# The FFN's up projection by one level of Strassen's scheme, with a separate down projection, in a float32 decoder layer on one core

## The chip, the cores and the metric

One Trainium2 chip; the kernel runs on one of its cores. The metric is the device time of one execution in microseconds (us). A core has five engines that work side by side, each through its own queue and strictly in that queue's order: TensorE (PE, with PEld for its loads of stationary tiles), VectorE (DVE), ScalarE (ACT), GpSimd (POOL) and SyncE (SP), which here only issues DMAs. SBUF holds tiles of 128 partitions; matmuls write to PSUM, which has banks of 512 float32 columns in a partition.

## The reference, cut to what matters

The reference is a decoder layer with two mixer branches, cross attention and a gated convolutional FFN, for 1024 tokens of 1024 channels, float32. The change touches the last part only (`D_FF` is 2816, so `w_up` is 1024 x 5632):

```python
def _conv_ffn(h, w_up, conv_w, conv_b, w_down):
    u = _causal_dwconv(h @ w_up, conv_w, conv_b)
    a, b = jnp.split(u, 2, axis=-1)
    return (jax.nn.gelu(a) * b) @ w_down
...
        h = _rmsnorm(x, f_norm_g[l])
        x = x + _conv_ffn(h, f_w_up[l], f_conv_w[l], f_conv_b[l], f_w_down[l])
    return _rmsnorm(x, final_norm_g)
```

The convolution is causal over three tokens, for each channel by itself.

## The kernel before

Activations lie channel-major: a tile has 128 channels in the partitions and the 1024 tokens (T) in the free dimension, so 1024 channels are 8 K tiles (KD). A float32 product is made of three passes of a faster type: both factors are split into a high part (a cast on ScalarE, L176) and a low part (the difference, on VectorE or GpSimd, L177), and a matmul group computes high x high, high x low and low x high (`gemm_part`, L202). One instruction takes a stationary tile of 128x128 and a moving tile of 128x512. `ntile` makes one 128-column tile of a product with K = 1024: 8 K tiles x 3 passes x 2 halves of the tokens, 48 matmuls. `load_w` loads a weight tile of 512 KB through SyncE's queue into WR and splits it into WH and WL (two buffers each) or into a pool that is passed in; its low parts go to VectorE and GpSimd in turn (`low`).

SBUF is shared out by pools that all stages take tiles from: S (24 tiles of 128x1024), R (4), Z (3), Y (18 of about 128x512), VV (4). PSUM has psM, two tiles of two banks, and psA, four of one bank.

The output projection of the attention and the second residual are in `resid` (L872): for each K tile n the projection, two additions to x2 (halves of the tokens), the scaled split of x2 into the FFN's moving tiles x2g (in S, R and pairs of Y), and the sum of squares for the norm. The norm's factor by token, r3, is not multiplied into x2g; it is computed while the first up tile runs (`rstd_col`, L229 on VectorE and L230 on GpSimd), broadcast over the partitions by matmuls (`bcast_col`, L236) and applied to each up tile as it leaves PSUM.

The FFN goes through 22 (NF) pairs of channel tiles, f of the first half and NF + f of the second. `up_conv` runs `ntile`, multiplies PSUM by rb3 (L1044, VectorE), starts the convolution on ScalarE (L1045) and adds its two other taps on VectorE (L1047). `ups` takes the gelu (L1057), multiplies the halves on GpSimd (L1059) and splits the product, the hidden tile. Hidden tiles stay in SBUF. Chunks of two hidden tiles (FCH) are followed by their share of the down projection (`downs`: `down_tile` and an addition of PSUM to x2, L1080), so that up and down tiles alternate; the down weights' splits lie in VV. The last four hidden tiles are taken with the final norm by token spans (`span_sum`, `span_norm`), the tail.

The kernel's instructions are handed to a scheduler (`schedule_with_timeline_sim=True`), which decides the order of each engine's queue before the kernel runs; the order of the code is only its input.

Of the kernel before, what the change touches and what calls it, by code (L numbers as in the profile page):

```python
# [10 lines left out]
F32 = mybir.dt.float32  # L11
# [8 lines left out]
P = 128  # L20
# [23 lines left out]
NZ = 3  # L44
# [3 lines left out]
# the order of the first part: p, r S5's parameters and runs; v values, g gates, j projections, m heads, s splits  # L48
# of the mLSTM; a merge of its share; y loads of S5's outputs
# [5 lines left out]
# the order of the cross attention's projections: k, v, q  # L55
# [30 lines left out]
def hybrid_layer(ctx: ExitStack, tc: tile.TileContext, a):  # L86
# [69 lines left out]
    # the tensor engine's clock rises with use: products of zeros until the first inputs are in  # L156
# [7 lines left out]
    class Halves:  # L164
        """Two [128, 512] tiles in the place of one [128, 1024]."""
# [30 lines left out]
    def gemm_part(ps, wk, xh, xl, width, first, last):  # L196
        """ps[:, :width] += w^T x for one K tile; wk = (hi, lo) stationary [128, 128]."""
        wh, wl = wk
        spans = [(s, min(s + 512, width)) for s in range(0, width, 512)]
        for lhsT, rhs, is_first, is_last in ((wh, xh, True, False), (wh, xl, False, False), (wl, xh, False, True)):  # L200
            for s, e in spans:
                PE.matmul(ps[:, s:e], lhsT, rhs[:, s:e], start=first and is_first, stop=last and is_last)  # L202
# [10 lines left out]
    def rstd_col(sq, n, out, more=()):  # L213
        """out[:, j] = (sum over partitions of sq at token j*128+p, / n + eps)^-1/2; sq: halves; more: further addends."""
        ntt = out.shape[1]
        t = small([P, 8], "ms", 2)
        if more:
            # a bank for each column, so that the last addend is all that is left at the end
# [6 lines left out]
        else:  # L225
            ps = psA()
# [5 lines left out]
    def bcast_col(cvec, halves):  # L232
        """halves[i][m, j*128+p] = cvec[p, 4i+j] for every m (PSUM banks)."""
# [5 lines left out]
    def rstd_bc(rcol, out):  # L239
        h = [psA(), psA()]  # L240
# [54 lines left out]
    for j in range(4):  # L295
# [3 lines left out]
        # block step reversed, so that x is (channel, step) rows in the order of the powers  # L299
# [12 lines left out]
    def acc_exp(dst, x, tmp):  # L312
        """dst = exp(x) to float32's accuracy; tmp: four slices of x's width and one of integers."""
# [22 lines left out]
    def sincos(cos_out, sin_out, f, t1, t2):  # L336
        """cos/sin of f turns, |f| a little over 1/2 at most, by half angles."""
# [7 lines left out]
    def cmul(e, re, im, ar, ai, br, bi, t1, t2):  # L345
        """(re, im) = (ar, ai) * (br, bi)"""
# [7 lines left out]
    # b and c, [128 = (group of pair, state), pair, channel]; the imaginary part of c negated  # L354
# [7 lines left out]
    # powers a^0 .. a^8: real, imaginary, negated imaginary part  # L362
# [25 lines left out]
    # turns of theta (m = 1) and of 8 theta (m = 8): leading part, small rest  # L388
# [33 lines left out]
    # input coefficient (a - 1) / lambda  # L422
# [33 lines left out]
    def s5_params(qi):  # L456
# [8 lines left out]
        # a^j b, j = 0..7, and conj(c a^j), j = 1..8  # L465
# [15 lines left out]
        # impulse response Re(c a^j b), with d at j = 0, to DRAM behind seven zero blocks  # L481
# [22 lines left out]
        # state to output, rows (real, imaginary) x state of one group  # L504
# [8 lines left out]
    def s5_run(qi, abt, es):  # L513
# [8 lines left out]
        # rotation by 8 theta per block  # L522
# [7 lines left out]
        # block inputs  # L530
# [7 lines left out]
        # rotate back to one phase, scan over blocks, rotate forward  # L538
# [25 lines left out]
        # outputs, [128 blocks, (step, channel)]  # L564
# [51 lines left out]
    def gate_rows():  # L616
# [48 lines left out]
        # emt = exp(-(bcum + M)) in ls, iw = exp(m_prev - M) in xf, w = exp(a + g - m_new) in ig, -M in cmax  # L665
# [48 lines left out]
        # chunk states, the normaliser as the last column  # L714
# [27 lines left out]
        # scores  # L742
# [6 lines left out]
        # output gates by token  # L749
# [6 lines left out]
        # numerators, with the denominator as the last column; gated numerators and their sums of squares  # L756
# [183 lines left out]
    def v_step(pv, k):  # L940
        """One K tile of the token-major values."""
# [81 lines left out]
    def alloc_x2(n):  # L1023
        if n < 4:
            return (S, R)[n // 2](F32R), (S, R)[n // 2](F32R)
        return Halves([Y(F32R), Y(F32R)]), Halves([Y(F32R), Y(F32R)])

    x2, x2g, sq2 = resid(a["w_o"], oT, lambda n: x1[n], "f_g", alloc_x2)
# [227 lines left out]
```

## Time and profile before

| | us |
|---|---|
| device time, three runs | 1744.49, 1749.63, 1749.22 |
| median | 1749.22 |
| span of the profiled execution | 1743.6 |
| mean time of L1044 (x44), L1059 (x22) | 1.224, 2.399 |
| load of an up weight tile, 512 KB | 3.3 |
| mean DMA rate over the span | 63 GB/s |

The page gives the span of the profiled execution, from its first instruction to its last, and no device time beside it; the fastest run is 0.9 us longer than this span, the median 5.6. In the rows below, a line is "start, duration, engine, line, operation, output<-inputs, shape, xcount", and square brackets hold how long the engine had idled and what released it. In rows of groups, the numbers behind the bar are busy microseconds in all, mean nanoseconds of one, and idle time just before them with what ended most of it. Such an idle time counts only on an engine that others wait for.

### The profile page before, as it was taken

The page shows a single profiled execution, that of the slowest core. Times are in us where ns is not written, and L with a number is a line of the kernel's source. Part 1 is how long each engine was busy: PE and PEld are TensorE (multiplying, and loading weights), DVE is VectorE, ACT ScalarE, POOL GpSimd, SP SyncE. Part 2 cuts the span into 40 slices and gives each one's busy share as a digit, 9 for nine tenths or more (in the row PEclk, how much of TensorE's full clock was granted, in tenths as well). Part 3 has the DMA queues.
Part 4 walks back from the last instruction along what each step waited for, and adds up shares of the span by engine and source line. Part 5 has one row for each costly group of instructions (what it writes and reads, how often), then busy time and mean ns, then how long its engine had stood idle before and what let it go on. Part 6 is the DMA issues. An engine that isn't in the chain of part 4 may idle for free. (4 is left out here: it accounts for less than half of the span.)

```text
span 1743.6 us, 20590 instructions
## 1 busy us (share of the span) xinstructions
PE 1711.3 (98%) x8435; PEld 1433.4 (82%) x8435; DVE 881.6 (51%) x1261; ACT 594.4 (34%) x895; POOL 351.5 (20%) x215
## 2 busy tenths in 40 slices
PE   9889999999999999999999999999999999999997
PEld 7788888888888888888888888888888888888887
DVE  8776766565243333623563545453453454454445
ACT  5345654544342222523452333222122122222223
POOL 2352323321022211000001122121121121121125
PEclk9899999999999999999999999999999999999999
DMA  5231321113111212223101111111111111111102
GB/s 182 88 93 39 99 72 55 45 57 112 44 61 43 84 62 97 97 80 115 61 1 49 48 51 59 48 45 53 49 36 61 48 36 61 49 37 61 49 12 97
DMA packets 46142, 110.59 MB, mean 63 GB/s; under 512 B 5024, under 2 KB 19040, under 8 KB 46048
## 3 DMA queue, kind: packets, MB, share of 16 engines
q1 hardware_dynamic: 42544, 101.24, 17.9%
q10 hardware_dynamic: 3504, 8.04, 1.3%
q8 instruction: 66, 1.08, 0.3%
q14 instruction: 28, 0.23, 0.0%
HBM read 100.35 MB, written 8.91 MB: 63 GB/s over the span
## 5 line engine op out<-in xcount | busy, mean ns | idle before, releaser
L202 PE MATMUL M<-S,WH 128*128 128x512 f32 (+1 forms) x2184 | 582.7, 384 | 0.0
L202 PEld LDWEIGHTS M<-S,WH 128*128 128x128 f32 x2184 | 403.5, 188 | 80.2 <-issue 0.3
L202 PE MATMUL M<-S,WL 128*128 128x512 f32 (+1 forms) x1124 | 347.9, 384 | 0.0
L176 ACT CAST WH<-WR 128x1024 fp32r<-128x1024 f32 (+2 forms) x143 | 137.2, 960 | 547.8 <-PE M L202 462.3
L177 POOL TENSOR_TENSOR WL<-WR,WH 128x1024 fp32r<-128x1024 f32 (+2 forms) x60 | 124.8, 2080 | 942.6 <-ACT WH L176 927.3
L202 PEld LDWEIGHTS M<-S,WL 128*128 128x128 f32 x1124 | 210.5, 188 | 40.8 <-DVE WL L177 0.2
L202 PE MATMUL M<-Y,WH 128*128 128x512 f32 x832 | 231.5, 393 | 0.0
L202 PE MATMUL M<-S,VV 128*128 128x512 f32 (+1 forms) x924 | 213.5, 390 | 0.0
L202 PEld LDWEIGHTS M<-S,VV 128*128 128x128 f32 x924 | 170.6, 188 | 40.5 <-DVE S L1080 2.0
L202 PEld LDWEIGHTS M<-Y,WH 128*128 128x128 f32 x832 | 156.2, 188 | 35.2
L1044 DVE TENSOR_TENSOR S<-M,Z 128x1024 f32<-128x1024 f32 x44 | 53.9, 1224 | 216.3 <-PE M L202 207.4
L177 DVE TENSOR_TENSOR WL<-WR,WH 128x1024 fp32r<-128x1024 f32 (+2 forms) x83 | 98.8, 1190 | 99.4 <-ACT WH L176 99.3
L1047 DVE SCALAR_TENSOR_TENSOR S<-S,cols,S 128x1023 f32<-128x1023 f32 x88 | 120.6, 1372 | 23.1 <-ACT S L1045 21.9
L1080 DVE TENSOR_TENSOR S<-S,M 128x512 f32<-128x512 f32 x144 | 93.1, 682 | 60.6 <-PE M L202 60.6
L202 PE MATMUL M<-Y,WL 128*128 128x512 f32 x352 | 109.6, 392 | 0.0
L202 PE MATMUL M<-R,WH 128*128 128x512 f32 x368 | 99.0, 389 | 0.0
L202 PEld LDWEIGHTS M<-R,WH 128*128 128x128 f32 x368 | 69.1, 188 | 14.3
L202 PEld LDWEIGHTS M<-Y,WL 128*128 128x128 f32 x352 | 66.0, 188 | 15.2
L176 ACT CAST S<-S 128x1024 fp32r<-128x1024 f32 x22 | 23.1, 1050 | 130.4 <-POOL S L1059 130.4
L1059 POOL TENSOR_TENSOR S<-S,S 128x1024 f32<-128x1024 f32 x22 | 52.8, 2399 | 64.6 <-DVE S L1047 64.6
L1045 ACT ACTIVATE S<-S,cols 128x1024 f32<-128x1024 f32 x44 | 54.8, 1245 | 31.6 <-DVE S L1044 31.6
L883 DVE TENSOR_TENSOR S<-S,M 128x512 f32<-128x512 f32 x32 | 20.6, 684 | 85.5 <-PE M L202 85.5
(397 smaller groups left out, 2124.1 us busy)
## 6 DMA issues: line engine op xcount, KB each, us to landing
WR<-in_w_up_dram SPq DMA_DIRECT2D x44, 512.0 KB, 3.3
WR<-in_w_in_dram SPq DMA_DIRECT2D x29, 512.0 KB, 3.3
WR<-in_w_down_dram SPq DMA_DIRECT2D x22, 512.0 KB, 3.2
Y<-Rd SPq DMA_DIRECT2D x16, 256.0 KB, 5.2
WR<-in_w_br_dram SPq DMA_DIRECT2D x16, 256.0 KB, 2.7
WR<-in_w_out_dram SPq DMA_DIRECT2D x8, 512.0 KB, 3.7
S<-in_xT_dram ACTq DMA_DIRECT2D x8, 512.0 KB, 3.3
WR<-in_w_q_dram SPq DMA_DIRECT2D x8, 512.0 KB, 3.3
```

The source lines that it names most:

```text
L176: A.copy(out=hi, in_=src)
L177: (lo_eng or V).tensor_tensor(out=lo, in0=src, in1=hi.bitcast(F32), op=ALU.subtract)
L202: PE.matmul(ps[:, s:e], lhsT, rhs[:, s:e], start=first and is_first, stop=last and is_last)
L883: V.tensor_tensor(out=xj, in0=xj, in1=ps[:, hs], op=ALU.add)
L1044: V.tensor_tensor(out=raw, in0=ps, in1=rb3, op=ALU.mult)
L1045: A.activation(out=acc, in_=raw, func=AF.Identity, scale=col("fcw", 3 * ct + 2), bias=col("fcb", ct))
L1047: V.scalar_tensor_tensor(out=acc[:, d_:], in0=raw[:, : T - d_], scalar=col("fcw", 3 * ct + 2 - d_), in1=acc[:, d_:], op0=ALU.mult, op1=ALU ...
L1059: G.tensor_tensor(out=gb, in0=ga, in1=gb, op=ALU.mult)
L1080: V.tensor_tensor(out=xj, in0=xj, in1=ps[:, 512 * j : 512 * j + 512], op=ALU.add)
```

## The change

Strassen's scheme in Winograd's form computes a 2x2 block product with seven products of blocks instead of eight, for more additions. Here the blocks are: the even and the odd K tiles (the inner dimension), the two channel tiles of a pair (f and NF + f), and the two halves of the tokens, H0 and H1. A pair, 96 matmuls before, is seven products of 12 (4 K tiles x 3 passes).

- The right factors X[1..7] of the products are made once from x2 (`factors_even`, `factors_odd`): differences of scaled tiles on VectorE and GpSimd, and the split of each. Product 1's lie in VV, product 5's in R, the others in S.
- The left factors are made for each pair from four blocks of weights: four sums on GpSimd (`sums`), casts on ScalarE and low parts on VectorE, or GpSimd for products 2 and 4 (`weights`). They are prepared seven products ahead; three of the seven slots are pairs of Y tiles, the others halves of WH and WL tiles. The host lays `w_up` out in these blocks.
- The products are combined as they leave PSUM (`product`): a copy on ScalarE, six VectorE passes that read PSUM, and the factor rb3 on VectorE for one quarter and on GpSimd for three (L1148, L1151). `finish` has the convolution, gelu and product of the halves, and writes the hidden tile to DRAM (Gd).
- x2 goes to DRAM (X2d) and comes back when the last pair begins. The down projection is a stage by itself behind all pairs, with hidden tiles and weights loaded one chunk ahead, in nine chunks of two and the unchanged tail.
- Z has six tiles, and the scratch memory of dynamic DMAs is set to 2048 bytes. All comments are gone.

```diff
-NZ = 3
+NZ = 6
...
+    def put(p, i, f, alloc):
+        hi, lo = HL(alloc)
+        A.copy(out=hi, in_=f)
+        (G if p in (1, 3, 5) else V).tensor_tensor(out=lo, in0=f, in1=hi.bitcast(F32), op=ALU.subtract)
+        X[p][i] = (hi, lo)
...
+    class Pair:
+        BANK = {1: 0, 2: 0, 6: 1, 7: 2, 4: 2, 5: 3, 3: 3}
...
+        def sums(self):
+            a11, a21, a22, a12 = self.r0[:, H0], self.r0[:, H1], self.r1[:, H0], self.r1[:, H1]
+            s1, s2, s3, s4 = [Y() for _ in range(4)]
+            G.tensor_tensor(out=s1, in0=a21, in1=a22, op=ALU.add)
+            G.tensor_tensor(out=s2, in0=s1, in1=a11, op=ALU.subtract)
+            G.tensor_tensor(out=s3, in0=a21, in1=a11, op=ALU.subtract)
+            G.tensor_tensor(out=s4, in0=a12, in1=s2, op=ALU.subtract)
+            self.src = {1: a11, 2: a12, 3: s4, 4: a22, 5: s1, 6: s2, 7: s3}
+
+        def weights(self, p):
+            k = wslot[0] = (wslot[0] + 1) % 7
+            if k in (1, 3, 5):
+                hi, lo = Y(F32R), Y(F32R)
+            else:
+                w = wp.tile([P, T], F32R, tag="WH" if k in (0, 4) else "WL", name=nm("W2"))
+                hi, lo = w[:, H0], w[:, H1]
+            A.copy(out=hi, in_=self.src[p])
+            (G if p in (2, 4) else V).tensor_tensor(out=lo, in0=self.src[p], in1=hi.bitcast(F32), op=ALU.subtract)
+            self.w[p] = (hi, lo)
...
+        def product(self, p):
+            ps = self.bank(self.BANK[p])
...
+            for i in range(4):
+                c = slice(i * P, (i + 1) * P)
+                xh, xl = X[p][i]
+                for lhsT, rhs, f, l in ((wh, xh, p in self.FRESH and i == 0, False), (wh, xl, False, False), (wl, xh, False, i == 3)):
+                    PE.matmul(ps, lhsT[:, c], rhs, start=f, stop=l, skip_group_check=True)
...
+            if p == 1:
+                left["s"] = Y()
+                A.copy(out=left["s"], in_=ps)
+            elif p == 6:
+                left["u2"] = Y()
+                V.tensor_tensor(out=left["u2"], in0=left["s"], in1=ps, op=ALU.add)
+            elif p == 2:
+                V.tensor_tensor(out=self.ra[:, H0], in0=ps, in1=rb3[:, H0], op=ALU.mult)
...
+                    V.tensor_tensor(out=self.rb[:, H1], in0=left["u3"], in1=ps, op=ALU.add)
...
+                    V.tensor_tensor(out=self.ra[:, H1], in0=left["u2"], in1=ps, op=ALU.add)
+                G.tensor_tensor(out=self.ra[:, H1], in0=self.ra[:, H1], in1=rb3[:, H1], op=ALU.mult)
+            if p == 4:
+                V.tensor_tensor(out=self.rb[:, H0], in0=left["u2"], in1=ps, op=ALU.add)
+                G.tensor_tensor(out=self.rb, in0=self.rb, in1=rb3, op=ALU.mult)
...
+            G.tensor_tensor(out=gb, in0=ga, in1=gb, op=ALU.mult)
+            nc.sync.dma_start(out=Gd[self.f], in_=gb)
...
+    STEADY = (1, 6, 7, 5, 2, 4, 3)
...
+    for k, (f, p) in enumerate(jobs):
+        pr = pairs[f]
+        if not pr.have:
+            if f + 2 < NF:
+                pairs[f + 2].load(S)
...
+        if len(pr.have) == 3 and f > 1:
+            for g in (f - 1,) if f > 2 else (0, 1):
+                pairs[g].finish()
+        pr.product(p)
+        weights(k + 7)
+        if k == 1:
+            rstd_col(sq2, D, r3, alloc=psM)
+        elif k == 2:
+            m = psM()
+            rstd_bc(r3, rb3, [m[:, H0], m[:, H1]])
...
+        downs(ws, gs)
+        if c == 0:
+            pairs[NF - 1].finish()
```

The scheduler orders both kernels' queues anew. Three places show how. (A name's number is the buffer; L numbers of the changed kernel are its own: L1120 the products' matmul, L1084 to 1087 the sums, L1098 a low part of weights, L1128, L1137 and L1142 reads of PSUM, L1148 and L1151 the factor rb3, L1157 the convolution, L1165 the product of the halves.) First TensorE around the broadcast of r3 (L236), before, inside the first up tile:

```order
L202 MATMUL M_7768<-Y_7445,WH_7764 128x512
L202 MATMUL M_7768<-Y_7446,WH_7764 128x512
L202 MATMUL M_7768<-Y_7447,WH_7764 128x512
L202 MATMUL M_7768<-Y_7448,WH_7764 128x512
L202 MATMUL M_7768<-Y_7445,WL_7765 128x512
L236 MATMUL A_7743<-ident,r_7674 128x128 x4
L236 MATMUL A_7744<-ident,r_7674 128x128 x4
L202 MATMUL M_7768<-Y_7446,WL_7765 128x512
```

The same place in the changed kernel's TensorE queue, inside a product of pair 0:

```order
L1120 MATMUL A_7814<-S_7791,W_1126_7768 128x512 x3
L1120 MATMUL A_7834<-S_7264,Y_7771 128x512 x2
L1120 MATMUL A_7834<-S_7264,Y_7772 128x512
L1120 MATMUL A_7834<-S_7425,Y_7771 128x512 x2
L1120 MATMUL A_7834<-S_7425,Y_7772 128x512
L236 MATMUL M_7889<-ident,r_7119 128x128 x8
L1120 MATMUL A_7834<-S_7586,Y_7771 128x512 x2
L1120 MATMUL A_7834<-S_7586,Y_7772 128x512
```

The broadcast stands in the middle of a group of matmuls in both. Second, GpSimd's queue in the middle of the FFN, before:

```order
L177 TENSOR_TENSOR WL_9713<-WR_9710,WH_9712 128x1024
L1059 TENSOR_TENSOR S_9626<-S_9564,S_9626 128x1024
L177 TENSOR_TENSOR WL_9961<-WR_9958,WH_9960 128x1024
L1059 TENSOR_TENSOR S_9766<-S_9704,S_9766 128x1024
L177 TENSOR_TENSOR VV_10033<-WR_10030,VV_10032 128x1024
```

GpSimd's queue in the changed kernel, the second part of a round of two pairs that repeats through the up stage:

```order
L1084 TENSOR_TENSOR Y_10062<-WR_9894,S_9895 128x512
L1098 TENSOR_TENSOR W_1527_10003<-S_9746,W_1527_10003 128x512
L1085 TENSOR_TENSOR Y_10063<-Y_10062,WR_9894 128x512
L1086 TENSOR_TENSOR Y_10064<-WR_9894 128x512
L1087 TENSOR_TENSOR Y_10065<-S_9895,Y_10063 128x512
L1165 TENSOR_TENSOR S_9967<-S_9962,S_9967 128x1024
L1098 TENSOR_TENSOR Y_10170<-S_9895,Y_10169 128x512
L1151 TENSOR_TENSOR Z_9900<-Z_9900,Z_7120 128x1024
L1098 TENSOR_TENSOR W_1554_10152<-S_9895,W_1554_10152 128x512
L1148 TENSOR_TENSOR Z_9899<-Z_9899,Z_7120 128x512
L1151 TENSOR_TENSOR Z_10047<-Z_10047,Z_7120 128x1024
L1148 TENSOR_TENSOR Z_10046<-Z_10046,Z_7120 128x512
```

Where GpSimd had low parts and one product of halves, it now has sums, low parts, factors and products of halves of two pairs in one queue, with the factors of both pairs at the end of the round. Third, VectorE's queue in the middle of the FFN, before:

```order
L1044 TENSOR_TENSOR S_8011<-M_7962,Z_7675 128x1024
L177 TENSOR_TENSOR WL_8099<-WR_8096,WH_8098 128x1024
L1047 SCALAR_TENSOR_TENSOR S_8012<-S_8011,cols,S_8012 128x1023
L1047 SCALAR_TENSOR_TENSOR S_8012<-S_8011,cols,S_8012 128x1022
L1044 TENSOR_TENSOR S_8073<-M_8024,Z_7675 128x1024
```

VectorE's queue in the changed kernel, in the same round of two pairs (A and M are PSUM):

```order
L1098 TENSOR_TENSOR W_1516_9923<-WR_9745,W_1516_9923 128x512
L1128 TENSOR_TENSOR Y_9938<-Y_9913,M_9898 128x512
L1098 TENSOR_TENSOR W_1522_9959<-Y_9917,W_1522_9959 128x512
L1098 TENSOR_TENSOR Y_9941<-Y_9916,Y_9940 128x512
L1137 TENSOR_TENSOR Y_9957<-Y_9938,M_9944 128x512
L1098 TENSOR_TENSOR Y_9987<-Y_9915,Y_9986 128x512
L1157 SCALAR_TENSOR_TENSOR S_9962<-Z_9750,cols,S_9962 128x1023
L1157 SCALAR_TENSOR_TENSOR S_9962<-Z_9750,cols,S_9962 128x1022
L1157 SCALAR_TENSOR_TENSOR S_9967<-Z_9751,cols,S_9967 128x1023
L1157 SCALAR_TENSOR_TENSOR S_9967<-Z_9751,cols,S_9967 128x1022
L1098 TENSOR_TENSOR W_1541_10070<-WR_9894,W_1541_10070 128x512
L1142 TENSOR_TENSOR Z_9900<-Y_9957,M_9944 128x512
```

Reads of PSUM, which had two passes of other work between them, now stand among low parts of the next pair's weights and, for both tiles of a pair at once, four convolution passes.

More of the change, by code (lines that the diff above doesn't have):

```diff
@@ new lines, in hybrid_layer, with weights, begin @@
+    pairs = [Pair(f) for f in range(NF)]
+    jobs = [(0, 1), (0, 5), (1, 1), (1, 5), (0, 2), (0, 3), (1, 2), (1, 3), (0, 7), (0, 6), (0, 4), (1, 7), (1, 6), (1, 4)]
+    jobs += [(f, p) for f in range(2, NF) for p in STEADY]
+    wslot = [6]
+    def weights(k):
+        if k < len(jobs):
+            f, p = jobs[k]
+            if not hasattr(pairs[f], "src"):
+                pairs[f].sums()
+            pairs[f].weights(p)
+    def begin():
+        for f in range(2):
+            pairs[f].load(Z)
+            pairs[f].sums()
+        for k in range(7):
+            weights(k)
```

204 lines of the change are left out of this document (137 added, 67 removed).

## The prediction

> **What bounds the kernel now.** I read the page's busy times first, then a table of windows by stage, then single rows of TensorE, VectorE and GpSimd inside the FFN stage.
>
> ```profile
> span 1743.6 us, 20590 instructions
> PE 1711.3 (98%) x8435; PEld 1433.4 (82%) x8435; DVE 881.6 (51%) x1261; ACT 594.4 (34%) x895; POOL 351.5 (20%) x215
> ```
>
> ```profile
> core 0: us, PE busy (x) PEld busy (x) DVE busy (x) ACT busy (x) POOL busy (x), PEclk, DMA share, GB/s
> 200.00:920.00 720.00, 716.29 (x3658) 606.55 (x3658) 343.18 (x533) 285.62 (x504) 115.45 (x79) 1.00 0.22 70
> 920.00:1015.90 95.90, 95.90 (x440) 79.83 (x439) 41.86 (x53) 29.91 (x44) 11.26 (x5) 1.00 0.15 50
> 1015.90:1681.80 665.90, 665.90 (x2898) 542.70 (x2897) 320.44 (x325) 165.24 (x150) 125.88 (x52) 1.00 0.15 49
> 1681.80:1743.60 61.80, 50.85 (x333) 46.10 (x331) 30.44 (x56) 20.29 (x41) 26.99 (x23) 0.94 0.19 69
> ```
>
> The columns are busy microseconds and instructions by engine, then the granted clock. The output projection (920 to 1015.9) and the FFN (to 1681.8) have TensorE busy for all of their 761.8 us at a clock of 1.00. VectorE is busy for 48% of the FFN and GpSimd for 19%. So matmuls set the time, and whatever removes matmuls gains at once, until another engine needs longer than what is left.
>
> **Matmuls: what goes and what comes.** Starts of groups of matmuls late in the FFN:
>
> ```profile
> 1659.80 1.07 PE L202 MATMUL M<-S,WH 128*128 128x512 f32 x4
> ...
> 1665.24 1.10 PE L202 MATMUL M<-Y,WH 128*128 128x512 f32 x4
> ...
> 1670.78 1.07 PE L202 MATMUL M<-S,WH 128*128 128x512 f32 x4
> ...
> 1681.76 5.71 PE L202 MATMUL A<-S,VV 128*128 128x512 f32 x24
> 1687.31 5.70 PE L202 MATMUL M<-S,VV 128*128 128x512 f32 x24
> ```
>
> One up tile of 48 matmuls takes 1670.78 - 1659.80 = 10.98 us, 0.2288 each. Its first 24, with moving tiles from S, take 5.44 (0.2267 each), its last 24, from Y, 5.54 (0.231). With stationary tiles in VV, 24 take 1687.31 - 1681.76 = 5.55 (0.231). So tiles in Y or VV cost 0.004 us a matmul.
>
> Before, 44 up tiles have 2112 matmuls: 2112 x 0.2288 = 483.2 us, 21.96 for a pair of tiles. After, 22 pairs of 7 products of 12 have 1848. Product 1 reads VV, products 6, 5 and 4 mostly have weights in Y: 4/7 x 0.231 + 3/7 x 0.2267 = 0.2292, so 423.6 us, **19.25 for a pair**. TensorE alone gains 59.6. The down projection keeps its 1056 matmuls; 912 of them trade weights in VV for WH, WL or S: 912 x (0.2267 - 0.231) = -3.8.
>
> **What VectorE and GpSimd must now do in those 19.25 us.** Prices:
>
> ```profile
> L1143 POOL TENSOR_TENSOR Z<-Z,Y 128x512 f32<-128x512 f32 x7 | 9.1, 1293 | 11.2 <-ACT Y L1139 10.8
> L1059 POOL TENSOR_TENSOR S<-S,S 128x1024 f32<-128x1024 f32 x22 | 52.8, 2399 | 64.6 <-DVE S L1047 64.6
> L1080 DVE TENSOR_TENSOR S<-S,M 128x512 f32<-128x512 f32 x144 | 93.1, 682 | 60.6 <-PE M L202 60.6
> 955.41 0.68 DVE L890 TENSOR_TENSOR Z<-Z,Y 128x512 f32<-128x512 f32 x1
> 1056.60 2.60 DVE L1047 SCALAR_TENSOR_TENSOR S<-S,cols,S 128x1023 f32<-128x1023 f32 x2 [0.18 <-ACT S L1045]
> L1045 ACT ACTIVATE S<-S,cols 128x1024 f32<-128x1024 f32 x44 | 54.8, 1245 | 31.6 <-DVE S L1044 31.6
> L176 ACT CAST S<-S 128x1024 fp32r<-128x1024 f32 x22 | 23.1, 1050 | 130.4 <-POOL S L1059 130.4
> ```
>
> GpSimd has, for a pair, seven passes of 512 (four sums L1084-1087, two low parts L1098, the factor L1148) at 1.293 and two of 1024 (L1151, L1165) at 2.399: 13.85 us. VectorE has five low parts at 0.68 and four convolution passes at 1.30, together 8.6, and six reads of PSUM at 0.682, 4.1: 12.7. ScalarE has seven casts of half of 1.050, a PSUM copy of about the same, two L1155 at 1.245 and a gelu of about as much: some 8. Each alone is below 19.25. But the first two do not run side by side:
>
> ```profile
> 942.00 0.75 DVE L255 SCALAR_TENSOR_TENSOR R<-S,cols,R 128x512 fp32r<-128x512 f32 x1
> 951.27 2.41 POOL L177 TENSOR_TENSOR WL<-WR,WH 128x1024 fp32r<-128x1024 f32 x1 [19.35 <-ACT WH L176]
> 952.03 2.19 DVE L255 SCALAR_TENSOR_TENSOR R<-S,cols,R 128x512 fp32r<-128x512 f32 x1 [0.20 <-ACT R L254]
> ...
> 1044.62 4.63 DVE L1047 SCALAR_TENSOR_TENSOR S<-S,cols,S 128x1023 f32<-128x1023 f32 x2 [1.76 <-ACT S L1045]
> 1044.70 3.47 POOL L177 TENSOR_TENSOR VV<-WR,VV 128x1024 fp32r<-128x1024 f32 x1
> ...
> 1091.94 1.28 DVE L1080 TENSOR_TENSOR S<-S,M 128x512 f32<-128x512 f32 x2
> 1092.16 2.41 POOL L1059 TENSOR_TENSOR S<-S,S 128x1024 f32<-128x1024 f32 x1 [3.49 <-DVE S L1047]
> 1093.97 1.28 DVE L1080 TENSOR_TENSOR S<-S,M 128x512 f32<-128x512 f32 x2 [0.75 <-PE M L202]
> ```
>
> A VectorE pass that takes 0.75 alone takes 2.19 when a GpSimd pass is under way, and ends 954.22 - 953.68 = 0.54 us after it. Two convolution passes that take 2.60 take 4.63 beside GpSimd; the GpSimd pass takes 3.47 in place of 2.41, and the second convolution pass ends 1049.25 - 1048.17 = 1.08 after it. They go one after the other. The reads of PSUM at 1091.94 and 1093.97, with one SBUF operand, are as short beside GpSimd as elsewhere, and GpSimd keeps its 2.41. So a VectorE pass with two SBUF operands and a GpSimd pass exclude each other. The part that excludes is 0.54 per 512 and 1.08 per 1023 columns on VectorE; on GpSimd, 1048.17 less the first convolution pass's end near 1045.90, 2.27 per 1024, which I halve to 1.13 for 512.
>
> For a pair: GpSimd 7 x 1.13 + 2 x 2.27 = 12.45, VectorE 5 x 0.54 + 4 x 1.08 = 7.02, **together 19.5**. That stands just above TensorE's 19.25: the shared resource and TensorE come to be nearly equal, with nothing left to hide a wait. The bounds are 19.5 (only the excluding parts) and 13.85 + 8.6 = 22.45 (whole durations). I take 19.5, since both pairs of rows show it.
>
> The Trainium skill, "SBUF — State Buffer", section "Who interferes with whom", speaks against this change: the shared pair of ports is an exclusive lock, given to the first for its whole instruction, while the other blocks fully. Taken at its word this makes 22.45 of a pair in place of 19.5. The rows agree on exclusion, with 2.19 for 0.75; but on a lock for the whole duration they say 0.54 and 1.08 after GpSimd's end where 0.75 and 1.30 would be due.
>
> **The up stage as a sum.** The excluding work starts in earnest when x2's seventh tile is ready, one tile of matmuls (10.98) less two reads of PSUM (0.68 each), about 9.5 us ahead of the first product. Entry, by the printed order: 15 GpSimd and 28 VectorE passes of 512 for the right factors, 15 x 1.13 + 28 x 0.54 = 32, and 8 for what is left of the first two pairs' weights. Then the weights of 20 pairs: (6 x 1.13 + 5 x 0.54) = 9.5 each, 190. Then 20.5 finishes of 10.0 (1.13 + 2 x 2.27 + 4 x 1.08), 205. Together 435, which ends 425.5 after the first product. That would cost TensorE 2 us against its 423.6. To it I add idle time of the pair of engines. At the end of a pair GpSimd's row L1148 stands for VectorE's read of product 3, then ScalarE's L1155 stands between that and the convolution, and in the printed order GpSimd has L1151 and L1148 together at the end of its two-pair round. Bounds: nothing, where other rows always fill it, and 0.68 + 1.29 + 1.245 = 3.2 where none do. I take the ScalarE pass alone, about 1.3 a pair: 22 x 1.3 = 28.6. **Up stage 454 us.**
>
> **Other edits.** At the entry, the broadcast of r3 stands in TensorE's row among products of pair 0 and waits for GpSimd's L230:
>
> ```profile
> 1007.04 1.64 POOL L230 TENSOR_TENSOR r<-ms,mhalf 128x8 f32<-128x8 f32 x1 [9.84 <-DVE ms L229]
> WR<-in_w_up_dram SPq DMA_DIRECT2D x44, 512.0 KB, 3.3
> ```
>
> Before, GpSimd idled 9.84 us ahead of L230. After, sums and low parts of two pairs are queued ahead of it, and behind the waiting L236 all products. In the printed order some 17 GpSimd rows stand between the last x2 tile's arrival and L230's result, by 1.13 to 1.29 each and 1.64 for L230 itself 19 to 24 us; TensorE comes to L236 after some 15.3. By this estimate TensorE waits 4 to 9 us, but the same GpSimd work is in the sum of 435 already, so it is not added again. Loads: 512 KB land in 3.3 us and a pair's are asked for two pairs ahead, about 38 us; the writes of hidden tiles ahead of them on SyncE's queue wait for L1165, and even a wait of one pair leaves 19 us. So nothing; without that cover up to 3.3 us a pair. The round trip of x2 has the up stage to hide in. The handover to the down stage, where WL's low part is queued on GpSimd behind L1151, bounds 0 and 4: I take 1. Three more Z tiles let earlier stages be ordered anew: at most the 720.00 - 716.29 = 3.7 us of idle TensorE there, either sign, taken as 0. The tail is the same code: 0.
>
> **Sum:** 454 - 483.2 - 3.8 + 1 = -32 us. Against the profiled span of 1743.6 that is 1711.6. The page gives no device time of that execution; the median of the runs, 1749.22, lies 5.6 above the span, the fastest 0.9. Against the median: **1717 us**, 1.8% faster. About 0.3% (5 us) is what a measurement of this kernel can tell from no change.
>
> **Rivals.**
> 1. *All of it hides behind TensorE.* VectorE's and GpSimd's passes interleave so that the excluding parts stay under 19.25, and only about 4 us of the entry shows: -59.6 - 3.8 + 4 = -59.4, 1690. For it: ScalarE and VectorE are far from full. Against it: 19.5 is already above. 0.15.
> 2. *The pair of engines excludes for whole durations, and becomes the bound.* Entry 15 x 1.293 + 28 x 0.68 + 9 = 47.4, weights 20 x 11.2 = 223, finishes 20.5 x 11.3 = 232: 502, less 9.5 is 492.5, so +9.3 - 3.8 + 1 = +6.5: 1756, and 1784 with the idle time of 28.6 on top. Its place is each pair's GpSimd round; it decides for slower from (483.2 + 2.8) / 22 = 22.1 us a pair. For it: 19.5 to 22.45 straddles that point. Against it: the 0.54 and 1.08. It is what the Trainium skill's rule above would give. 0.15.
> 3. *Order of queues.* VectorE's reads of PSUM stand behind low parts (L1128 between two L1098) that wait for GpSimd's sums, and TensorE waits for the bank. Bounds 0 and one GpSimd pass, 1.29, a pair; with one VectorE pass, 0.68, it is 22 x 0.68 = +15 on the forecast: 1732. 0.15.
>
> The change does what it says: 264 fewer matmuls is exact, and no rival.
>
> **How the numbers follow.** Forecast 0.55 with 1717; rivals 0.15 each. The range 1690 to 1756 takes in rivals 1 and 3 and the lower half of 2: the upper half of 2 and some beyond either end, about 0.2, are left out. Faster by over 0.3% (under 1744): forecast 0.52 of its 0.55, rival 1, rival 3's 0.12: 0.79. Slower (over 1754): rival 2's 0.12 and 0.02 of the forecast: 0.14. Within: 0.07.
>
> **What would show it.** In the profile after: TensorE's matmuls of the products at 0.229 each (right) or longer; a pair's period near 20.6 us (forecast), 19.3 (rival 1), 22 or more (rival 2); TensorE's idle time in the up stage near 30 us, put down to low parts of weights on GpSimd or VectorE; GpSimd passes longer than 1.29 and 2.40 beside two-operand passes of VectorE, and reads of PSUM still at 0.68; one stall of 4 to 9 us at the broadcast of r3; the down stage without idle TensorE. I am wrong if TensorE's idle time is small while GpSimd is over 85% busy, or if it waits for PSUM banks rather than weights.

## The result, and the profile after

The changed kernel takes 1769.51 us (median of 4 runs, 1761.13 to 1771.16); the kernel before, run beside it, 1748.02. The ratio is 1.0117, with a 95% interval of 1.0090 to 1.0144: **slower by 1.2%**, where 1.8% faster was forecast. The profiled execution has a span of 1768.0 us and a device time of 1769.82; the forecast span was 1711.6.

The page of the changed kernel, its span and busy times:

```profile
span 1768.0 us, 20923 instructions
PE 1682.3 (95%) x8171; PEld 1403.6 (79%) x8171; DVE 1105.7 (63%) x1434; ACT 655.4 (37%) x1051; POOL 709.1 (40%) x400
```

TensorE has 264 matmuls less, yet its share of the span fell from 98% to 95%; GpSimd's busy time has doubled. The up stage of the changed kernel, from its first product to the first down matmul, as a window (busy time of PE, PEld, DVE, ACT, POOL, then granted clock, DMA share, GB/s):

```profile
998.40:1501.46 503.06, 457.24 (x1881) 365.46 (x1880) 404.51 (x333) 179.24 (x254) 404.15 (x203) 0.94 0.23 78
```

What TensorE waited for there (total, times, longest), in the same kernel:

```profile
PE A L1120 <- DVE W L1098: 19.9, 9, 3.6
PE M L1120 <- DVE Z L1142: 16.0, 5, 3.7
PE A L1120 <- ACT Y L1097: 6.8, 1, 6.8
PE M L1120 <- DVE Y L1137: 2.3, 1, 2.3
PE M L1120 <- ACT Y L1125: 0.9, 1, 0.9
```

The stage takes 503 us where 454 were forecast and the matmuls need 423.6 (427.4 with the 3.8 for r3's). Two losses of different kind stand in the window's row: 503.06 - 457.24 = 45.8 us in which TensorE waits, and a granted clock of 0.94, which is 0.06 x 503 = 30 us of matmuls at reduced clock (457.24 is 30 more than 427.4). Before, the FFN had neither.

The clock falls around the end of a wait. TensorE in the changed kernel around one of them, and windows over the same stretch (the last three columns are granted clock, DMA share and GB/s):

```profile
1253.56 1.57 PE L1120 MATMUL A<-R,Y 128*128 128x512 f32 x6
1258.80 4.61 PE L1120 MATMUL M<-S,Y 128*128 128x512 f32 x12 [3.67 <-DVE Z L1142]
1263.25 1.55 PE L1120 MATMUL A<-R,Y 128*128 128x512 f32 x6
1264.63 2.93 PE L1120 MATMUL A<-S,W 128*128 128x512 f32 x12
```

```profile
1254.00:1259.00 5.00, 1.33 (x6) 0.76 (x5) 4.96 (x5) 1.23 (x3) 5.00 (x3) 1.00 0.01 4
1259.60:1262.90 3.30, 3.30 (x9) 2.60 (x8) 3.14 (x5) 0.62 (x1) 1.41 (x2) 0.50 0.82 304
1263.00:1268.00 5.00, 5.00 (x23) 4.07 (x22) 1.77 (x3) 0.40 (x1) 3.29 (x2) 1.00 0.00 0
```

Twelve matmuls that take 2.93 us at full clock take 4.61 behind a wait of 3.67, since the clock is 0.50 in the second window. So TensorE loses more by a wait than the wait's own length; whether the round gets longer by the second part too is not shown here (see e4).

What VectorE did meanwhile (timeline of the changed kernel):

```profile
1245.76 0.67 DVE L1137 TENSOR_TENSOR Y<-Y,M 128x512 f32<-128x512 f32 x1
1246.35 1.18 DVE L1098 TENSOR_TENSOR Y<-Y,Y 128x512 fp32r<-128x512 f32 x1
1247.46 9.02 DVE L1157 SCALAR_TENSOR_TENSOR S<-Z,cols,S 128x1023 f32<-128x1023 f32 x4
1256.40 1.74 DVE L1098 TENSOR_TENSOR W<-WR,W 128x512 fp32r<-128x512 f32 x1
1258.07 0.67 DVE L1142 TENSOR_TENSOR Z<-Y,M 128x512 f32<-128x512 f32 x1
```

GpSimd beside the same four passes of VectorE, one round earlier in the same kernel:

```profile
1207.47 2.28 POOL L1085 TENSOR_TENSOR Y<-Y,WR 128x512 f32<-128x512 f32 x1
1209.72 2.28 POOL L1086 TENSOR_TENSOR Y<-WR 128x512 f32<-128x512 f32 x1
1211.96 2.28 POOL L1087 TENSOR_TENSOR Y<-S,Y 128x512 f32<-128x512 f32 x1
```

The product that waits (M<-S,Y: a weight in Y, an even pair's two-bank tile M) is released by L1142, a read of M that is short (0.67) but queued behind four convolution passes and a low part. L1142 reads product 5 from one bank of M, and the waiting product 4 accumulates in the other. The convolution passes take 2.26 each in place of 1.30, and GpSimd's passes beside them 2.28 in place of 1.29: the two engines take turns.

### The profile page after: what moved, and what is told of

Its sections match the earlier page's. It is cut to its first block, busy times and chain, and to the rows that moved or that the text cites. A ratio compares the mean times of both kernels' runs of the same rounds, so it can differ in the third digit from the quotient of the medians.

```text
span 1768.0 us, 20923 instructions
## 1 busy us (share of the span) xinstructions
PE 1682.3 (95%) x8171; PEld 1403.6 (79%) x8171; DVE 1105.7 (63%) x1434; ACT 655.4 (37%) x1051; POOL 709.1 (40%) x400
## 4 chain that ended last, share of the span: by engine, by line
PE 72%; DVE 16%; issue 5%; POOL 3%; ACT 3%; DMA 1%; SPq 0%; POOLq 0%; DVEq 0%; ACTq 0%
PE M L202 37%; PE A L1120 7%; PE M L1120 6%; PE M L1260 5%; PE A L1260 5%; DVE S L1157 4%; DVE W L1098 3%; PE M L991 1%; PE A L1016 1%; PE A L202 1%; PE A L948 1%; POOL Z L1148 1%; DVE Y L1098 1%; PE M L288 1%; ACT S L1155 1%
## 5 line engine op out<-in xcount | busy, mean ns | idle before, releaser
L202 PE MATMUL M<-S,WH 128*128 128x512 f32 (+1 forms) x1832 | 489.4, 383 | 1.2 <-DVE R L789 1.2
L202 PEld LDWEIGHTS M<-S,WH 128*128 128x128 f32 x1832 | 338.3, 189 | 67.0 <-ACT WH L176 1.6
L1157 DVE SCALAR_TENSOR_TENSOR S<-Z,cols,S 128x1023 f32<-128x1023 f32 (+1 forms) x88 | 184.5, 2113 | 17.0 <-ACT S L1155 16.4
L1120 PE MATMUL M<-S,W 128*128 128x512 f32 x396 | 98.0, 395 | 2.3 <-DVE Y L1137 2.3
L1120 PE MATMUL A<-S,W 128*128 128x512 f32 x396 | 98.2, 394 | 0.0
L1120 PE MATMUL M<-S,Y 128*128 128x512 f32 x276 | 76.3, 431 | 16.9 <-DVE Z L1142 16.0
L1120 PEld LDWEIGHTS M<-S,W 128*128 128x128 f32 x396 | 75.0, 190 | 19.5 <-issue 2.7
L1120 PEld LDWEIGHTS A<-S,W 128*128 128x128 f32 x396 | 75.6, 191 | 17.2
L1120 PEld LDWEIGHTS M<-S,Y 128*128 128x128 f32 x276 | 56.8, 208 | 33.1 <-DVE Z L1142 18.3
L1120 PE MATMUL A<-S,Y 128*128 128x512 f32 x252 | 67.5, 400 | 0.0
L1120 PE MATMUL A<-VV,W 128*128 128x512 f32 x144 | 47.9, 483 | 19.9 <-DVE W L1098 19.9
L1165 POOL TENSOR_TENSOR S<-S,S 128x1024 f32<-128x1024 f32 x22 | 59.7, 2712 | 8.9 <-DVE S L1157 7.7
L1098 DVE TENSOR_TENSOR Y<-Y,Y 128x512 fp32r<-128x512 f32 x45 | 61.4, 1367 | 1.4 <-ACT Y L1097 1.2
L1148 POOL TENSOR_TENSOR Z<-Z,Z 128x512 f32<-128x512 f32 x22 | 44.6, 2029 | 43.3 <-DVE Z L1147 43.3
L1098 DVE TENSOR_TENSOR W<-Y,W 128x512 fp32r<-128x512 f32 x43 | 54.3, 1263 | 8.0 <-ACT W L1097 7.1
```

The source lines that it names most:

```text
L1098: (G if p in (2, 4) else V).tensor_tensor(out=lo, in0=self.src[p], in1=hi.bitcast(F32), op=ALU.subtract)
L1120: PE.matmul(ps, lhsT[:, c], rhs, start=f, stop=l, skip_group_check=True)
L1148: G.tensor_tensor(out=self.ra[:, H1], in0=self.ra[:, H1], in1=rb3[:, H1], op=ALU.mult)
L1157: V.scalar_tensor_tensor(out=acc[:, d_:], in0=raw[:, : T - d_], scalar=col("fcw", 3 * ct + 2 - d_), in1=acc[:, d_:], op0=ALU.mult, op1=ALU ...
L1165: G.tensor_tensor(out=gb, in0=ga, in1=gb, op=ALU.mult)
```

## The experiments

All start from the changed kernel. "Up" is the up stage from its first product to its last, "busy" TensorE's busy time in it, "clock" the granted clock in it, from the windows of each profiled execution.

| run | edit | median us | ratio to before [95%] | up | busy | clock |
|---|---|---|---|---|---|---|
| after | none | 1769.5 | 1.0117 [1.0090, 1.0144] | 503 | 457 | 0.94 |
| e1 | sums left out | 1701.5 | 0.9745 [0.9723, 0.9766] | 438 | 433 | 1.00 |
| e2 | sums on VectorE | 1715.8 | 0.9824 [0.9807, 0.9840] | 450 | 435 | 0.99 |
| e3 | factor on VectorE | 1710.1 | 0.9792 [0.9773, 0.9811] | 445 | 434 | 0.99 |
| e4 | 80 matmuls more | 1768.1 | 1.0130 [1.0100, 1.0159] | 506 | 470 | 0.97 |
| e5 | second tap left out | 1724.5 | 0.9865 [0.9850, 0.9879] | 463 | 439 | 0.99 |
| e6 | first tap, one operand | 1740.0 | 0.9951 [0.9934, 0.9967] | 478 | 446 | 0.97 |
| e7 | sums and factor on VectorE | 1712.3 | 0.9797 [0.9782, 0.9812] | 445 | 434 | 0.99 |
| e8 | e3, and the right factors' low parts | 1704.5 | 0.9752 [0.9737, 0.9766] | 439 | 432 | 1.00 |
| e9 | L1148 alone on VectorE | 1762.7 | 1.0089 [1.0064, 1.0114] | 497 | 451 | 0.96 |
| e10 | L1151 alone on VectorE | 1752.6 | 1.0033 [1.0020, 1.0045] | 490 | 451 | 0.96 |
| e11 | 40 matmuls more | 1787.4 | 1.0229 [1.0199, 1.0258] | 522 | 469 | 0.93 |
| e12 | e8, and the first two pairs' sums | 1707.4 | 0.9772 [0.9750, 0.9794] | 441 | 434 | 0.99 |
| e13 | product 5 through ScalarE | 1746.0 | 0.9991 [0.9981, 1.0001] | 480 | 444 | 0.98 |

The kernel before, run again beside each group of them, had medians of 1746.0 to 1748.2, so a difference of some 2 us between two rows says nothing.

The first question was whether the amount of work that VectorE and GpSimd cannot do side by side sets the time, or VectorE's own queue, or a chain that doesn't depend on load.

**e1**, the sums left out:

```diff
-            G.tensor_tensor(out=s1, in0=a21, in1=a22, op=ALU.add)
...
-            self.src = {1: a11, 2: a12, 3: s4, 4: a22, 5: s1, 6: s2, 7: s3}
+            self.src = {1: a11, 2: a12, 3: a12, 4: a22, 5: a21, 6: a11, 7: a21}
```

> The four GpSimd sums of each pair are left out (raw weight blocks stand in their place, so the hidden tiles are not the reference's); all else stays. Theory A (passes that exclude each other on VectorE and GpSimd are too long for TensorE's time): 19.5 us of excluding work a pair becomes 15.0, below TensorE's 19.25, so most of the 46 us of TensorE idle time in the up stage and of its half-clock stretches go: 1685 to 1710 us. Theory B (VectorE's own queue, with its reads of PSUM behind other passes, sets the time): VectorE keeps all its passes: 1750 or more. Theory C (fixed chains of waits from product to read to factor to product, whatever the load): within 5 us of 1769.

1701.45 us, as theory A had it. TensorE is busy for 433 of 438 us at a clock of 1.00.

**e2**, the sums on VectorE (four lines of this kind), and **e3**, the factor on VectorE:

```diff
-            G.tensor_tensor(out=s1, in0=a21, in1=a22, op=ALU.add)
+            V.tensor_tensor(out=s1, in0=a21, in1=a22, op=ALU.add)
```

```diff
-                G.tensor_tensor(out=self.ra[:, H1], in0=self.ra[:, H1], in1=rb3[:, H1], op=ALU.mult)
+                V.tensor_tensor(out=self.ra[:, H1], in0=self.ra[:, H1], in1=rb3[:, H1], op=ALU.mult)
...
-                G.tensor_tensor(out=self.rb, in0=self.rb, in1=rb3, op=ALU.mult)
+                V.tensor_tensor(out=self.rb, in0=self.rb, in1=rb3, op=ALU.mult)
```

> The four sums of each pair go from GpSimd to VectorE. Theory A: an excluding part of 512 columns is 1.13 us on GpSimd and 0.54 on VectorE, so a pair's excluding work falls from 19.5 to 17.1, under TensorE's 19.25: 1700 to 1735 us. Theory B: VectorE gets four passes of 0.68 more a pair, 22 x 2.7 = 60 us: 1800 or more. Theory C: within 5 us of 1769.

> The factor rb3 (one pass of 512 and one of 1024 a pair) goes from GpSimd to VectorE. Theory A: excluding work 19.5 to 17.7 us a pair: 1705 to 1740 us. Theory B: VectorE gets 2.0 us more a pair: 1800 or more. Theory C: the chain from the last product through the factor to the convolution gets shorter by some 0.6 and 1.1 us, at most 22 x 1 us: 1747 to 1769.

1715.81 and 1710.08 us. In the changed kernel's up stage VectorE was as busy as GpSimd (404.5 and 404.2 us in the window above), and giving it more passes made the kernel 54 and 59 us faster, which speaks against theories B and C. TensorE's waits in e3's up stage:

```profile
PE A L1120 <- ACT Y L1097: 6.8, 1, 6.8
PE M L1120 <- DVE Y L1137: 2.4, 1, 2.4
PE M L1120 <- DVE Z L1142: 1.2, 1, 1.2
PE A L1120 <- DVE W L1098: 0.7, 1, 0.7
```

The 19.9 and 16.0 us are down to 0.7 and 1.2. What is left is the entry. The same product in two successive rounds of two pairs shows the pace (TensorE, e3):

```profile
1195.15 2.94 PE L1120 MATMUL M<-S,Y 128*128 128x512 f32 x12
...
1233.81 1.38 PE L1120 MATMUL M<-S,Y 128*128 128x512 f32 x5
```

38.66 us for two pairs, 19.33 for one: TensorE's own time, forecast as 19.25.

**e4**, matmuls of no use ahead of product 1 of odd pairs:

```diff
             wh, wl = self.w[p]
+            if p == 1 and self.f > 1 and self.f % 2:
+                for _ in range(8):
+                    PE.matmul(ps, wh[:, :P], X[1][0][0], start=True, stop=True, skip_group_check=True)
```

> Eight matmuls of no use (overwritten by the product that follows) stand ahead of product 1 of each odd pair from 3 on, where TensorE waits 1.4 to 3.6 us for a low part of weights: 80 matmuls, 18.2 us of work. Theory D (a wait of TensorE above some 2 us is followed by 3.4 or 6.8 us at half clock): the work falls into waits of about 23 us in all, five of the half-clock stretches (3.41 to 6.83 us each, half of which is lost) go: 1750 to 1766 us, with mean clock above 0.974. Rival (waits have no such price, the half-clock stretches come from elsewhere): nothing gained, 1769 to 1787, clock as before.

1768.1 us, between the two: 18 us of extra matmuls cost nothing that can be told, and the clock in the up stage rose from 0.94 to 0.97. But the waits did not go; they moved. e4's waits (L1145 is here what L1142 is in the others):

```profile
PE M L1123 <- DVE Z L1145: 19.6, 9, 2.3
PE M L1123 <- DVE Y L1140: 6.8, 5, 2.3
```

So TensorE isn't what sets the length of a round, and the run doesn't isolate the price of the clock.

All three of e1 to e3 lightened GpSimd. **e5** leaves GpSimd as it is and takes passes from VectorE; **e6** leaves the number of passes on both and takes an SBUF operand away:

```diff
-            for d_ in range(1, 3):
+            for d_ in range(1, 2):
```

```diff
-            for d_ in range(1, 3):
-                V.scalar_tensor_tensor(out=acc[:, d_:], in0=raw[:, : T - d_], scalar=col("fcw", 3 * ct + 2 - d_),
-                                       in1=acc[:, d_:], op0=ALU.mult, op1=ALU.add)
+            V.tensor_scalar(out=acc[:, 1:], in0=raw[:, : T - 1], scalar1=col("fcw", 3 * ct + 1), scalar2=1.0, op0=ALU.mult, op1=ALU.mult)
+            V.scalar_tensor_tensor(out=acc[:, 2:], in0=raw[:, : T - 2], scalar=col("fcw", 3 * ct),
+                                   in1=acc[:, 2:], op0=ALU.mult, op1=ALU.add)
```

> The convolution's second added tap (one VectorE pass of 1022 columns for each channel tile) is left out, so the output is not the reference's; no GpSimd pass changes. Theory A (passes exclude each other): 19.5 less 2 x 1.08 is 17.3 us a pair, about what the factor's move gave: 1698 to 1720 us. Rival G (GpSimd's own queue and load set the time, the runs so far having lightened it every time): nothing of GpSimd's changes: 1750 or more.

> The convolution's first added tap (1023 columns) is written as a pass with one SBUF operand (a product with a column, the addition left out, so the output is not the reference's); VectorE has as many passes as before, GpSimd too. Theory A: only passes with two SBUF operands exclude GpSimd's, 17.3 us a pair: 1698 to 1722 us, and the new pass takes the same beside GpSimd as alone. Rival (the number of passes, or either engine's load, counts, whatever the operands): 1750 or more. If the new pass excludes GpSimd too, its time is stretched in the trace as the old one's was, and the total stays near 1769.

e5 took 1724.52 us, 45 less with GpSimd's passes unchanged, so rival G falls (the size is 4 us above the expected range). e6 took 1739.97, neither as expected. VectorE's rows in e6 say why:

```profile
1204.48 1.78 DVE L1156 TENSOR_SCALAR S<-Z,cols 128x1023 f32<-128x1023 f32 x1
...
1227.29 0.75 DVE L1156 TENSOR_SCALAR S<-Z,cols 128x1023 f32<-128x1023 f32 x1
```

Alone the new pass takes 0.75, little over half the old one's 1.30; beside GpSimd it takes 1.78. It excludes GpSimd's passes too, though for less time: some 0.6 in place of 1.08, so about 18.5 us a pair. The Trainium skill, "SBUF — State Buffer", section "Who interferes with whom", names this: it lists `tensor_scalar`, the operation of the new pass, among those that can enter a two-port mode and then contend with GpSimd. The 0.75 and 1.78 agree. So e6 was no pass without exclusion, but a smaller amount of it, and 1740 lies between 1769 and e3's 1710 accordingly.

**e7** joins e2's and e3's edits; **e8** adds to e3's:

```diff
-        (G if p in (1, 3, 5) else V).tensor_tensor(out=lo, in0=f, in1=hi.bitcast(F32), op=ALU.subtract)
+        V.tensor_tensor(out=lo, in0=f, in1=hi.bitcast(F32), op=ALU.subtract)
```

> Sums and factor rb3 both go to VectorE: excluding work 15.3 us a pair, VectorE's own passes 17.4. Theory A: TensorE bounds the up stage already with the factor moved, so what is left is the entry (a wait of 6.8 us and 10.24 at half clock) and the down stage: within 8 us of 1710, 1700 to 1715. Rival B' (VectorE's own 17.4 us with its waits now is the bound): 1725 or more. Rival (excluding work still costs at 17.7): 1680 to 1697.

> The factor rb3 and the low parts of the right factors (12 passes in products 1, 3 and 5) on VectorE. Theory A: the entry's excluding work falls by 12 x 0.59 = 7 us, so the wait of 6.8 us at the second product and part of its 10.24 us at half clock go: 1698 to 1707 us. Rival (the entry waits for the chain from the last tile of x2, not for excluding work): within 3 us of 1710.

1712.3 and 1704.53 us. Beyond e3, less excluding work in the rounds brings nothing, since TensorE bounds them; less of it at the entry does: the wait of 6.8 us became 3.0. **e8 is the fastest kernel that computes the whole layer**, 2.5% faster than the kernel before. **e12** went on with the entry (V for the four sums where `self.f < 2`):

> The factor rb3, the right factors' low parts and the first two pairs' weight sums (eight passes) on VectorE. Theory A: eight passes less of 0.59, 4.7 us less of excluding work at the entry: 1698 to 1704 us. Rival (the entry now waits for the chain from the last tile of x2): within 2 us of 1704.5.

1707.43 us: nothing gained, neither theory's range; its entry still waits 3.6 us.

Next, whether the moved passes count by amount or by place. **e9** and **e10** each take one of e3's two edits:

> Of the factor rb3 only the pass of 512 behind product 3 (L1148) goes to VectorE: it stands in the chain from a pair's last product to its convolution. Theory A (the amount of excluding work): 19.5 less 0.59 a pair, about a third of what moving both gave (59 us): 1745 to 1760 us. Theory C' (the round's chain through L1148, for which GpSimd stands idle, matters more than the amount): most of what moving both gave, 1735 or less.

> Of the factor rb3 only the pass of 1024 (L1151) goes to VectorE; L1148 stays on GpSimd. Theory A: 19.5 less 1.19 a pair, two thirds of 59 us: 1722 to 1740. Theory C': the chain through L1148 is as long as before: 1750 or more.

1762.71 and 1752.57 us: 7 and 17 us less than the changed kernel. Both lie above theory A's ranges. e9 contradicts theory C' (1735 or less), but e10's time is the one that C' gave (1750 or more), so neither theory holds as it stood; and e9's 7 us are hardly clear of noise, since its interval and the changed kernel's overlap. Together the two gains are 24 us where both edits at once gave 59. The amount counts, yet not in a straight line. Long waits stay in both (nine of 3.5 to 3.9 us in e9's up stage, four of 3.8 to 3.9 in e10's) and half-clock stretches with them (the clock is 0.96). That the two losses end together once the rounds fit TensorE's time is a reading of these runs, not shown by one.

**e11** is e4 with `range(4)`:

> As with the eight matmuls of no use, but four (0.9 us) ahead of product 1 of each odd pair from 3 on, so that a wait of 2.6 us there becomes 1.7 and one of 1.4 becomes 0.5. Theory D' (the half-clock stretches that follow long waits lengthen the round): fewer of them, and a shorter time, 1755 to 1765 us. Rival (the round is set by the excluding passes and the chain through them, and the half clock falls into time that TensorE would have waited anyway): 1766 to 1773, with fewer half-clock stretches too.

1787.4 us, worse than either. The scheduler's order moved with the edit, and a wait of 3.9 us for the same read of PSUM (L1145 here) stands in nearly every round; e11's TensorE and clock around one:

```profile
1211.36 2.93 PE L1123 MATMUL M<-S,Y 128*128 128x512 f32 x6 [3.91 <-DVE Z L1145]
...
1259.08 3.35 PE L1123 MATMUL M<-S,Y 128*128 128x512 f32 x7 [3.88 <-DVE Z L1145]
```

```profile
1257.80:1264.60 6.80, 5.52 (x13) 4.36 (x14) 5.48 (x8) 0.62 (x1) 3.97 (x2) 0.50 0.37 136
```

A round is 1259.08 - 1211.36 = 47.7 us, of which two pairs' matmuls and four more need 39.4. The run was of no use for its question.

It pointed to the read that is queued behind the convolution. **e13** takes product 5 of even pairs out of PSUM by ScalarE, so that product 4 no longer waits for it:

```diff
-            elif p in (5, 3) and 6 not in self.have:
+            elif p in (5, 3) and 6 not in self.have or p == 5 and self.f > 1 and self.f % 2 == 0:
                 left[p] = Y()
                 A.copy(out=left[p], in_=ps)
...
-                    G.tensor_tensor(out=self.rb[:, H1], in0=left["u3"], in1=left.pop(5), op=ALU.add)
+                    (V if self.f > 1 else G).tensor_tensor(out=self.rb[:, H1], in0=left["u3"], in1=left.pop(5), op=ALU.add)
```

> In even pairs from 2 on, product 5 is copied out of PSUM by ScalarE and added on VectorE from SBUF (L1142's place), so that product 4, which shares the two-bank tile, no longer waits for a VectorE pass that is queued behind four convolution passes. The excluding work grows by 0.54 in every second pair, ScalarE gets 0.58 there. Theory Q (the order of VectorE's queue together with the shared PSUM tile makes waits, and each long wait is followed by 3.4 or 6.8 us at half clock): the 16 to 18 us of waits for L1142 and their half-clock stretches go, unless the wait moves to the low part ahead of product 1: 1735 to 1760 us. Theory A alone (only the amount of excluding work sets the round): 1769 to 1778.

1746.04 us, 23 less with slightly more excluding work, as theory Q had it. The waits in its up stage are many, but short:

```profile
PE A L1120 <- ACT Y L1097: 11.7, 4, 6.8
PE A L1120 <- DVE W L1098: 9.8, 6, 1.8
PE M L1120 <- ACT Y L1125: 9.5, 6, 2.4
```

The waits for L1142 are gone, those for L1098 went from 19.9 (longest 3.6) to 9.8 (longest 1.8), and the clock from 0.94 to 0.98. So the order of VectorE's queue, with a PSUM tile of two banks of which one waits for the reading of the other, is a cause beside the amount.

The traces split a pair's time into these two causes. Between product 1 of pair 4 and product 1 of pair 20, 16 pairs, the table gives the time of a pair, the part of it in which a GpSimd pass or a VectorE pass other than a read of PSUM was under way (overlaps counted once), and the part in which neither was:

| run | a pair, us | excluding passes | neither |
|---|---|---|---|
| after | 22.6 | 20.2 | 2.4 |
| e4 | 22.6 | 20.2 | 2.3 |
| e9 | 22.0 | 19.7 | 2.3 |
| e10 | 22.0 | 19.1 | 2.9 |
| e13 | 21.3 | 20.9 | 0.4 |
| e3 | 19.4 | 18.6 | 0.8 |

e13 raises the amount a little and takes away most of the idle time of the two engines. e10 takes 1.1 us of the amount away, but half of that comes back as idle time. In e3 TensorE has no wait in these 16 pairs.

## Why the prediction was wrong

Point by point:

- **Matmuls.** Right: 19.33 us for a pair where nothing waits (e3), against 19.25.
- **The prices of exclusion.** Nearly right. Four convolution passes beside GpSimd took 9.02, 2.26 each, against 1.08 + 1.13 = 2.21; a low part in turn with a GpSimd pass of 512 takes 1.74 against 0.54 + 1.13 = 1.67. So 19.5 us a pair was some 3% low, not the 15% of whole durations (rival 2). The Trainium skill, "SBUF — State Buffer", section "Who interferes with whom", states the lock for the whole instruction where it speaks of VectorE's two-port modes; of passes with two SBUF inputs, as these are, it says that they contend, which the rows bear out. That GpSimd's passes are the dear ones, with about twice the exclusion for the same columns, is what e2, e3 and e8 live from.
- **The step that failed** is the up stage's sum, 19.5 us of excluding work a pair and, for the idle time of the two engines, "I take the ScalarE pass alone, about 1.3 a pair: 22 x 1.3 = 28.6". Measured, a pair took 22.6 us in place of 20.8: 20.2 of excluding work and 2.4 of idle time (the table above). Over 22 pairs that is some 39 of the 49 us by which the stage is over its forecast. The larger miss is the idle time, and it is not the ScalarE pass alone. In the four pairs from 1258.80 to the same product at 1347.83, 4.0 of the 8.4 us of idle time end right behind L1147, a read that stood waiting for a product of TensorE:

```profile
1271.47 0.69 DVE L1147 TENSOR_TENSOR Z<-Y,M 128x512 f32<-128x512 f32 x1 [3.18 <-PE M L1120]
1314.09 0.69 DVE L1147 TENSOR_TENSOR Z<-Y,M 128x512 f32<-128x512 f32 x1 [2.75 <-PE M L1120]
```

  The first of these products was late: some 10 us before it TensorE had waited 3.67 us itself and then run at half clock. So each side stands waiting for the other in turn, and neither TensorE nor the two engines are full. The sum let the rest of a round overlap perfectly, and put what a wait does to the clock at nothing without a reason: 46 us of waits and 30 of reduced clock stand beside TensorE's 427. The same four pairs by TensorE:

```profile
1347.83 1.70 PE L1120 MATMUL M<-S,Y 128*128 128x512 f32 x4 [3.72 <-DVE Z L1142]
```

  89.0 us, 22.3 a pair, against the breakeven of 22.1 that rival 2 gave: 77.0 of matmuls, some 7.7 of waits (3.72, and 2.58 and 1.42 ahead of product 1), and the rest mostly half clock.
- **Rival 3** named the mechanism, a read of PSUM behind other passes of VectorE's queue, and priced it at 15 us, with "one VectorE pass, 0.68" a pair. L1142 alone cost 16.0 in waits, four of 3.7 and one of 1.2, since it stands behind four stretched convolution passes and a low part, not behind one low part. e13 shows 23 us for it. The outcome, slower than before, lies between rival 2's two prices, 1756 and 1784, by another way: nearly the forecast's amount, more idle time, half clock. Before, three passes (a low part and two convolution passes) stand between the two reads of the printed queue, not two, and TensorE did not wait for any read in the FFN.
- **The signs that it named.** It would be wrong, it said, if TensorE "waits for PSUM banks rather than weights". This came in part: of the waits listed above 26.7 us were for weights and 19.2 for PSUM.
- **The entry.** A wait of 6.8 us came, within 4 to 9, but at the second product, not at the broadcast of r3; the prediction had not added it to the sum, and it brought 10.2 us at half clock. The chain in the changed kernel:

```profile
1001.15 5.08 DVE L1038 TENSOR_TENSOR S<-Y,S 128x512 fp32r<-128x512 f32 x3
1006.16 1.27 DVE L1218 TENSOR_TENSOR S<-S,M 128x512 f32<-128x512 f32 x2
...
1006.87 0.72 ACT L254 ACTIVATE S<-S,cols 128x512 fp32r<-128x512 f32 x1 [7.58 <-DVE S L1218]
1007.50 1.64 ACT L1097 CAST Y<-Y 128x512 fp32r<-128x512 f32 x3
...
1008.15 1.22 PE L1120 MATMUL A<-R,Y 128*128 128x512 f32 x2 [6.79 <-ACT Y L1097]
```

  Low parts of right factors, stretched to 1.7 each, hold up the read of the last output-projection tile on VectorE; ScalarE stands for it, and the weight's cast behind it. e8, with GpSimd's share of the right factors' low parts moved to VectorE, cut the wait to 3.0.
- **Other terms.** The nine down chunks took 1705.99 - 1501.46 = 204.5 us, where the forecast amounts to some 196.8 (864 x 0.231 = 199.6, less 3.8 for cheaper stationary tiles, and 1 for the handover): 5.9 us of waits for L1262's additions outweighed the cheaper tiles. The up stage began 998.40 against 993.87 before, 4.5 later and a little beyond the 3.7 that was allowed for reordered earlier stages. The tail is within 0.2. The prediction's window of the output projection, 920 to 1015.90, takes in the FFN's first 22 us, which begin at 993.87; TensorE is busy throughout on both sides, and no term rests on it.

So the forecast named the right bound, the pair of engines just above TensorE, and with 1.8 to 4.5 us a pair less of their work (e3, e1) the gain that was forecast (and more) is there. What stays open is how much of the 76 us the clock costs by itself: no run kept the waits and spared the clock.

## What to carry to other kernels

When a change leaves TensorE and a shared pair of engines within a few per cent of each other, don't add the two amounts up and stop: a read of PSUM that stands behind long passes in an in-order queue makes TensorE wait, the late product makes the pair wait in turn, and neither is full (22.6 us a pair where 20.2 and 19.3 were needed). Where VectorE and GpSimd both could do a pass, compare what it keeps the other from, and not how busy each is: here an fp32 pass of 512 columns on GpSimd kept VectorE out for about 1.13 us and one on VectorE kept GpSimd out for 0.54, and moving passes from GpSimd to an equally busy VectorE gained 54 and 59 us. Look for reads that free a PSUM tile, and keep long elementwise passes out of their way.

## What the runs showed of the hardware that was not expected

- Around the end of a wait of TensorE the granted clock often was 0.50 for 3.4 or 6.8 us, as in the windows above. The changed kernel's eleven waits from 2.26 to 6.79 us in the up stage each had such a stretch (10.2 us long at the 6.79), which began 2.0 to 5.0 us after the wait did; its six waits of 0.9 to 1.5 us had none. In e4 six of nine waits of 2.2 to 2.3 had one. Over the up stages of the changed kernel and its 13 variants the shortest wait with one was 1.76 us (e10) and the longest without 3.53 (e9), so the length alone does not decide. The eleven starts lie whole multiples of 3.41 us apart (1259.56 and 1286.86, for one); whether a wait's place on that grid decides was not tested. The Trainium skill, "TensorE: Matmul & The Clock Gate", section "Why this matters for your kernels", advises against gaps above about 3 us; here shorter ones were enough.
- A VectorE pass with one SBUF operand and a scalar ran 1023 columns in 0.75 us, and excluded GpSimd (1.78 beside it), where passes with one operand in PSUM stayed within 0.67 to 0.69 through the whole up stage.
